# A log-sum-exp scan bound by its transfers: an opening store, a tail in rows, and no GpSimd drains

## Chip, cores, metric

One core of one Trainium2 chip. The metric is the device time of one execution in microseconds (us), lower is better.

## The reference

```python
x: (8, 4096, 2048) float32
out[:, 0, :] = x[:, 0, :]
for t in range(1, S):
    mx = np.maximum(out[:, t-1, :], x[:, t, :])
    out[:, t, :] = mx + np.log(np.exp(out[:, t-1, :] - mx) + np.exp(x[:, t, :] - mx))
```

It is a running log-sum-exp along the second axis. The kernel computes Exp, a running sum, and Ln. 268 MB are read and 268 MB written.

## The kernel before

The data go through in 64 tiles of 4 MB: 128 partitions, 4 consecutive rows of 2048 values in each (32 KB). Six buffers rotate. For every tile SyncE issues the load, ScalarE does Exp in two column halves, VectorE adds up the rows of each partition, TensorE multiplies by a triangle of ones for the sums of the partitions above and by a matrix that carries the last sum to the next tile, VectorE joins them, ScalarE does Ln and issues the store. Loads go through SyncE's DMA queue (the SP queue below), stores through ScalarE's (the ACT queue).

```python
@block.sync
def _(sp):
    def load(src, n):
        sp.dma_start(out=ti[n][:], in_=src).then_inc(loaded[n], 16)
    sp.dma_start(out=ti[0][:, 0:2, :], in_=x_v[0][:, 0:2, :]).then_inc(top, 16)
    sp.dma_start(out=ti[0][:, 2:R, :], in_=x_v[0][:, 2:R, :]).then_inc(loaded[0], 16)
    for n in range(1, NI):
        load(x_v[n], n)
    ...            # a loop: take(sp, stored[n], 16), then load the next tile into buffer n
    for n in range(NT - NI, NT):
        take(sp, stored[n % NI], 32 if n >= NT - 2 else 16)
```

`take` waits for a count on a semaphore and subtracts it. ScalarE's program, with its tail:

```python
take(act, top, 16)
act.activation(ti[0][:, 0:2, :], ti[0][:, 0:2, :], ACT.Exp)
exp(0, 0, slice(2, R))
exp(0, 1, slice(2, R))
...                # a loop of turns of six tiles: exp(n, 0), exp(n, 1), ln(n-1, 0), ln(n-1, 1), store(n-1)
for n in range(first + 1, NT):
    up, turn = n - 1, n - 1 - first
    exp(n, 0)
    if n < NT - 1:
        exp(n, 1)
    ln(up, 0, turn)
    if n == NT - 1:
        store(up, o_v[up], turn, 0)          # column half 0 of tile 62
        exp(n, 1)
    ln(up, 1, turn)
    store(up, o_v[up], turn, 1 if n == NT - 1 else None)
for h in range(2):                            # tile 63 in column halves
    ln(NT - 1, h, NT - 1 - first)
    store(NT - 1, o_v[NT - 1], NT - 1 - first, h)
settle(NT - first)
```

The softmax here doesn't subtract the row's maximum and nothing guards it: scores larger than these inputs give would overflow.

## Time and profile before

| | before |
|---|---|
| median, first three runs | 1250.71 us (1250.57 to 1251.23) |
| span of the profiled run | 1249.0 us |
| VectorE, ScalarE, TensorE busy | 82%, 73%, 52% |
| DMA | 537 MB, 430 GB/s, the DMA row 9 or more from the first slice to the 39th |

The prediction below shows the lines. The DMA share of a window can be above 1, as a packet counts with its whole duration where it starts. A DMA's semaphore goes up by 16, one step for each engine; the trace has the times of these steps, which I call landings, and they show how far the sixteen engines are apart. Neither they nor the packet records carry an engine's number: that it is one and the same engine that lands last from tile to tile (I call it the late engine), and that it is never idle, is read from how the times follow each other. And the chain of waits that the page gives ends at the last Ln, since a transfer is not an instruction: for a kernel bound by transfers it says little.

### The profile page before, as it was taken

To read this page: it belongs to the slowest core of one execution; us is meant where nothing else is said; L and a number is where in the kernel's file an instruction comes from. 1 tells how busy PE (TensorE), PEld (TensorE's weight loads), DVE (VectorE), ACT (ScalarE), POOL (GpSimd) and SP (SyncE) were. 2 spreads that over 40 slices of the span, in tenths; PEclk is the share of its full clock that TensorE was granted. 3 is DMA by queue.
4 is the path that set the end of the run, shared out by engine and by line. 5 is a ranking of instruction groups with operands and counts; after the bars stand their busy time and mean duration, and the time that the engine had idled before them with its cause. 6 is when DMAs were issued, how large, how long until landed. Compare 5 with 4: busy or idle time off the path is not lost. (4 is left out here: it accounts for less than half of the span.)

```text
span 1249.0 us, 3456 instructions
## 1 busy us (share of the span) xinstructions
PE 650.8 (52%) x960; PEld 215.3 (17%) x960; DVE 1023.0 (82%) x512; ACT 907.2 (73%) x258; POOL 1.1 (0%) x8
## 2 busy tenths in 40 slices
PE   3556455554566545655455544565545564465541
PEld 1112111111112111211111111121111121111110
DVE  4999978778787787887878878778787787877873
ACT  5897866867768677686776866867768677686774
POOL 0000000000000000000000000000000000000000
PEclk9897778786887868778778786777878878678785
DMA  9999999999999999999999999999999999999998
GB/s 403 420 436 430 433 430 437 433 431 434 430 436 434 431 433 430 437 434 430 434 430 436 436 430 434 430 436 437 428 434 431 436 436 429 434 430 436 436 430 354
DMA packets 20409, 537.01 MB, mean 430 GB/s; under 512 B 2096, under 2 KB 2096, under 8 KB 4144
## 3 DMA queue, kind: packets, MB, share of 16 engines
q1 hardware_dynamic: 9360, 268.44, 49.9%
q10 hardware_dynamic: 11040, 268.44, 49.9%
q8 instruction: 7, 0.11, 0.0%
q14 instruction: 2, 0.02, 0.0%
HBM read 268.44 MB, written 268.44 MB: 430 GB/s over the span
## 5 line engine op out<-in xcount | busy, mean ns | idle before, releaser
L136 ACT ACTIVATE ti<-ti 128x4096 f32<-128x4096 f32 (+1 forms) x128 | 452.6, 3582 | 310.2 <-ACTq L59 304.2
L232 DVE TENSOR_TENSOR ti<-ti 128x1024 f32<-128x1024 f32 x384 | 464.7, 1224 | 200.0 <-ACT ti L136 191.3
L241 DVE TENSOR_TENSOR ti<-ti,ps 128x4096 f32<-128x4096 f32 x128 | 560.0, 4416 | 9.4 <-PE ps L208 9.0
L208 PE MATMUL ps<-ti,before 128*128 128x512 f32 x512 | 380.4, 895 | 342.6 <-DVE ti L232 342.1
L142 ACT ACTIVATE ti<-ti 128x4096 f32<-128x4096 f32 x128 | 455.4, 3602 | 11.5 <-PE ps L197 6.0
L197 PE MATMUL ps<-ti,last 128*128 128x512 f32 x448 | 270.6, 735 | 234.2 <-DVE ti L241 234.2
L208 PEld LDWEIGHTS ps<-ti,before 128*128 128x128 f32 x512 | 128.7, 279 | 609.0 <-DVE ti L232 500.9
L197 PEld LDWEIGHTS ps<-ti,last 128*128 128x128 f32 x448 | 86.6, 214 | 401.8 <-DVE ti L241 334.7
L159 ACT ACTIVATE ti<-ti 128x4096 f32<-128x4096 f32 x1 | 3.6, 3616 | 6.5 <-ACTq L59 6.5
L32 ACT ACT_TABLE_LOAD x1 | 1.3, 1283 | 0.8 <-PEq L274 0.8
L103 POOL TENSOR_SCALAR_AFFINE_SELECT last<-last 128x128 f32<-128x128 f32 x1 | 0.3, 296 | 0.0
L98 POOL TENSOR_SCALAR_AFFINE_SELECT before<-before 128x128 f32<-128x128 f32 x1 | 0.3, 295 | 0.1
L95 POOL MEMSET last<- 128x128 f32 x1 | 0.2, 206 | 0.0
L94 POOL MEMSET before<- 128x128 f32 x1 | 0.2, 205 | 0.5 <-SPq L77 0.5
L274 POOL MEMSET const-bfloat16-1.0<- 128x1 bf16 x1 | 0.1, 103 | 0.0
L274 POOL MEMSET const-uint8-127<- 128x1 uint8 x1 | 0.1, 103 | 0.0
L274 POOL MEMSET const-float32-0.0<- 128x1 f32 x1 | 0.1, 99 | 0.3 <-issue 0.3
L274 POOL MEMSET const-float32-1.0<- 128x1 f32 x1 | 0.1, 99 | 0.0
## 6 DMA issues: line engine op xcount, KB each, us to landing
ti<-in_x_dram SPq DMA_DIRECT2D x63, 4096.0 KB, 38.4
out_dram<-ti ACTq DMA_DIRECT2D x62, 4096.0 KB, 44.0
out_dram<-ti ACTq DMA_DIRECT2D x4, 2048.0 KB, 12.9
ti<-in_x_dram SPq DMA_DIRECT2D x2, 2048.0 KB, 9.7
```

What stands on the lines that cost most here:

```text
L32: nc.scalar.preload_act_table_set("natural_log_exp_and_others")
L94: g.memset(before[:], 1.0).then_inc(ones, 1)
L98: g.affine_select(out=before[:], in_=before[:], compare_op=mybir.AluOpType.is_ge, fill=0.0, base=-1, pattern=[[1, P]], channel_multiplier= ...
L103: g.affine_select(out=last[:], in_=last[:], compare_op=mybir.AluOpType.is_ge, fill=0.0, base=-(P - 1), pattern=[[0, P]], channel_multiplier=1,
L136: act.activation(t[:, rows, half(h)], t[:, rows, half(h)], ACT.Exp).then_inc(exps[h], 1)
L142: act.activation(t[:, :, half(h)], t[:, :, half(h)], ACT.Ln)._wait_ge(carried[h], turn + 1).then_inc(logs, 1)
L159: act.activation(ti[0][:, 0:2, :], ti[0][:, 0:2, :], ACT.Exp)
L197: m = pe.matmul(ps[(n + 1) % 2][:, sl], last[:], ti[n % NI][:, R - 1, sl], start=True, stop=False, skip_group_check=True,)
L208: m = pe.matmul(ps[n % 2][:, sl], before[:], ti[n % NI][:, R - 1, sl], start=n % NBLK == 0, stop=True, skip_group_check=True,)
L232: a = dve.tensor_add(t[:, r, half(h)], t[:, r - 1, half(h)], t[:, r, half(h)])
L241: dve.tensor_add(t[:, :, half(h)], t[:, :, half(h)], ps[n % 2][:, half(h)].unsqueeze(1).to_broadcast([P, R, HALF]),)._wait_ge(ahead[h], n ...
L274: nc = _bacc.Bacc("TRN2", target_bir_lowering=False, num_devices=1)
```

## The change

The intent: let the ACT queue's first use happen at the head with sixteen elements, so that the first tile's store doesn't pay for it; give the last two tiles larger packets and earlier issues; drop the drains of GpSimd.

```diff
+    LAST = [slice(0, 1), slice(1, 2), slice(2, R)]
-    with tc.tile_critical():
+    with tc.tile_critical(no_gpsimd_drain=True):
-        with nc.Block() as block:
+        with nc.Block(no_gpsimd_drain=True) as block:
 ...
-                    take(sp, stored[n % NI], 32 if n >= NT - 2 else 16)
+                    take(sp, stored[n % NI], 16 * (len(LAST) if n == NT - 1 else 1))
 ...
             def _(act):
+                with nc.allow_non_contiguous_dma(reason="one element per DMA engine"):
+                    act.dma_start(
+                        out=o_v[0][0:16, 0, 0:1], in_=nc.const_aps.tensor(0.0, [16, 1], f32)
+                    ).then_inc(warm, 16)
 ...
                 take(act, top, 16)
+                take(act, warm, 16)
 ...
                 for n in range(first + 1, NT):
-                    ...                       # the tail shown above
+                    for h in range(2):
+                        exp(n, h)
+                    for h in range(2):
+                        ln(n - 1, h, n - 1 - first)
+                    store(n - 1, o_v[n - 1], 2 * (n - first))
+
+                turn = NT - 1 - first
+                ln(NT - 1, 0, turn)
+                done = 2 * turn + 1
+                for rows in LAST:
+                    ln(NT - 1, 1, turn, rows)
+                    done += 1
+                    store(NT - 1, o_v[NT - 1], done, rows)
+                settle(NT - first, done)
```

`store` takes rows instead of a column half. TensorE's program is not touched.

More of the change, by code (lines that the diff above doesn't have):

```diff
@@ L75, in take @@
         event(engine, [(s, n)], [(s, "sem-sub-imm", n)])
-    with tc.tile_critical():
+    with tc.tile_critical(no_gpsimd_drain=True):
         def sems(name, n):
             return [nc.alloc_semaphore(f"{name}{i}") for i in range(n)]
-        ones, shaped, logs, top = (
-            sems(s, 1)[0] for s in ("ones", "shaped", "logs", "top")
+        ones, shaped, logs, top, warm = (
+            sems(s, 1)[0] for s in ("ones", "shaped", "logs", "top", "warm")
         )
@@ L138, in exp, with ln, store, settle @@
                     ).then_inc(exps[h], 1)
-                def ln(n, h, turn):
+                def ln(n, h, turn, rows=slice(0, R)):
                     t = ti[n % NI]
                     act.activation(
-                        t[:, :, half(h)], t[:, :, half(h)], ACT.Ln
+                        t[:, rows, half(h)], t[:, rows, half(h)], ACT.Ln
                     )._wait_ge(carried[h], turn + 1).then_inc(logs, 1)
-                def store(n, dst, turn, h=None):
-                    cols = slice(0, D) if h is None else half(h)
-                    act.wait_ge(logs, 2 * turn + (2 if h is None else h + 1))
+                def store(n, dst, done, rows=slice(0, R)):
+                    act.wait_ge(logs, done)
                     act.dma_start(
-                        out=dst[:, :, cols], in_=ti[n % NI][:, :, cols]
+                        out=dst[:, rows, :], in_=ti[n % NI][:, rows, :]
                     ).then_inc(stored[n % NI], 16)
-                def settle(turns):
+                def settle(turns, done):
                     take(act, carried[0], turns)
                     take(act, carried[1], turns)
-                    take(act, logs, 2 * turns)
+                    take(act, logs, done)
                 take(act, top, 16)
+                take(act, warm, 16)
                 act.activation(ti[0][:, 0:2, :], ti[0][:, 0:2, :], ACT.Exp)
@@ L168, in _ @@
                         ln(n - 1, 1, n - 1)
-                        store(n - 1, o_v[bass.ds(j * NI + (n - 1), 1)][0], n - 1)
-                    settle(NI)
+                        store(n - 1, o_v[bass.ds(j * NI + (n - 1), 1)][0], 2 * n)
+                    settle(NI, 2 * NI)
                 first = turns * NI
                 for n in range(first + 1, NT):
-                    up, turn = n - 1, n - 1 - first
-                    exp(n, 0)
-                    if n < NT - 1:
-                        exp(n, 1)
-                    ln(up, 0, turn)
-                    if n == NT - 1:
-                        store(up, o_v[up], turn, 0)
-                        exp(n, 1)
-                    ln(up, 1, turn)
-                    store(up, o_v[up], turn, 1 if n == NT - 1 else None)
-                for h in range(2):
-                    ln(NT - 1, h, NT - 1 - first)
-                    store(NT - 1, o_v[NT - 1], NT - 1 - first, h)
-                settle(NT - first)
+                    for h in range(2):
[11 more added lines that the diff above has]
+                settle(NT - first, done)
             @block.tensor
```

## The prediction

> **What bounds the kernel now.** I read the page's strip of slices first, then the engines' busy shares, the DMA windows at head and tail, ScalarE's timeline at the tail and the issue list.
>
> ```profile
> PE 650.8 (52%) x960; PEld 215.3 (17%) x960; DVE 1023.0 (82%) x512; ACT 907.2 (73%) x258; POOL 1.1 (0%) x8
> ...
> DMA  9999999999999999999999999999999999999998
> GB/s 403 420 436 430 433 430 437 433 431 434 430 436 434 431 433 430 437 434 430 434 430 436 436 430 434 430 436 437 428 434 431 436 436 429 434 430 436 436 430 354
> DMA packets 20409, 537.01 MB, mean 430 GB/s; under 512 B 2096, under 2 KB 2096, under 8 KB 4144
> ```
>
> No compute engine is full, while the DMA row is 9 everywhere and the rate stands at 430 to 437 GB/s from the third slice to the 39th. 537 MB must pass and the change keeps every byte of it, so only the places where the rate falls short can give anything: the first two slices (403, 420) and the last (354). The row "under 8 KB" counts the pieces that matter at the tail: 4144 less 2096 is 2048 packets of 4 KB.
>
> The windows around the first store of a tile (ScalarE issues it at 38.46 us); the last two columns are DMA share and GB/s:
>
> ```profile
> 39.00:40.00 1.00, 0.82 (x2) 0.49 (x3) 1.00 (x2) 1.00 (x1) 0.00 (x0) 1.00 1.21 524
> 40.00:41.00 1.00, 1.00 (x3) 0.19 (x1) 1.00 (x1) 1.00 (x1) 0.00 (x0) 1.00 1.31 524
> 41.00:42.00 1.00, 0.16 (x1) 0.00 (x0) 1.00 (x1) 1.00 (x1) 0.00 (x0) 1.00 1.51 426
> 42.00:43.00 1.00, 0.00 (x0) 0.00 (x0) 1.00 (x1) 1.00 (x2) 0.00 (x0) 1.00 0.31 98
> ```
>
> A packet is counted in the window where it starts, so a window jumps between about 200 and 524; the ratio of the columns is what to read. A share of 1.21 normally buys 524 GB/s. The next three windows spend 3.13 where (524 + 426 + 98) / 524 x 1.21 = 2.42 would do: 0.71 us of all sixteen engines is lost. In the trace's packet records the loads of 32 KB in flight there take 1.3 to 2.0 us instead of 1.21, before the first store packet of the ACT queue starts; summed over 16 engines the excess is 0.70 us. No later store shows this. The only other such place is the very start of the SP queue at 2.0 to 3.5 us: first packets of 16 KB take 1.1 to 1.3 us instead of 0.61, 0.66 us per engine. So each queue's first use costs about 0.7 us of DMA time.
>
> The end of the run:
>
> ```profile
> 1230.00:1243.00 13.00, 0.00 (x0) 0.00 (x0) 2.41 (x1) 5.44 (x2) 0.00 (x0) 0.50 1.02 421
> 1243.00:1244.00 1.00, 0.00 (x0) 0.00 (x0) 0.00 (x0) 0.00 (x0) 0.00 (x0) 0.50 0.83 340
> 1244.00:1245.00 1.00, 0.00 (x0) 0.00 (x0) 0.00 (x0) 0.00 (x0) 0.00 (x0) 0.50 0.43 176
> 1245.00:1246.00 1.00, 0.00 (x0) 0.00 (x0) 0.00 (x0) 0.00 (x0) 0.00 (x0) 0.50 0.06 25
> 1246.00:1247.00 1.00, 0.00 (x0) 0.00 (x0) 0.00 (x0) 0.00 (x0) 0.00 (x0) 0.50 0.06 25
> 1247.00:1248.00 1.00, 0.00 (x0) 0.00 (x0) 0.00 (x0) 0.00 (x0) 0.00 (x0) 0.50 0.02 8
> ```
>
> A share of 0.06 is one engine in sixteen: from 1245.2 to 1247.3 a single DMA engine still writes. The sixteen increments of the last store's semaphore, in the trace, arrive at 1243.71 to 1245.47 for fifteen engines and at 1247.66 for one, and that one was 0.4 us behind the median at 8 us, 1.0 at 180, 2.1 at 760 and 3.0 at 1218. It is never idle between its first packet and 1247.33, so it is the critical path: its bytes, its stalls, and 1.7 us of semaphore and closing barriers up to the span of 1249.0.
>
> Is the last Ln on that path? ScalarE at the tail, and the issues:
>
> ```profile
> 1216.36 3.62 ACT L136 ACTIVATE ti<-ti 128x4096 f32<-128x4096 f32 x1 [0.71 <-ACT ti L142]
> 1219.88 3.60 ACT L142 ACTIVATE ti<-ti 128x4096 f32<-128x4096 f32 x1
> 1223.51 0.54 ACTq L149 DMA_DIRECT2D out_dram<-ti  x1
> 1228.21 3.62 ACT L142 ACTIVATE ti<-ti 128x4096 f32<-128x4096 f32 x1 [4.73 <-PEq L59]
> 1231.86 0.54 ACTq L149 DMA_DIRECT2D out_dram<-ti  x1
> 1232.54 3.62 ACT L142 ACTIVATE ti<-ti 128x4096 f32<-128x4096 f32 x1 [0.71 <-PEq L59]
> 1236.18 0.54 ACTq L149 DMA_DIRECT2D out_dram<-ti  x1
> ...
> out_dram<-ti ACTq DMA_DIRECT2D x4, 2048.0 KB, 12.9
> ```
>
> The last store leaves at 1236.18 and lands 11.5 us later, though 2.1 MB at 421 GB/s are 5.0 us. It stood some 6 us in line, behind bytes already queued. So the last Ln has slack.
>
> **What the Trainium skill says.** "Perfetto Trace Analysis", section "What 'DMA-bound' means", lists specific DMA engines as a first kind of bound; the windows at 25 GB/s show just that. "DMA: Bandwidth & Descriptors", section "Why a DMA increments its semaphore by 16 and not by 1", says that the engines of a transfer finish independently and only the full count means landed; the spread 1243.71 to 1247.66 agrees. Its section "Why small descriptors are slow (HBM only)" gives a fixed cost per packet; in the trace 4 KB packets follow each other every 155.3 ns, those of 16 KB every 608 and of 32 KB every 1210, that is 155.3, 152.1 and 151.3 ns for each 4 KB, which agrees: some 4 ns a packet. I found nothing in it on the first use of a queue.
>
> **The change part by part.**
>
> 1. *Tail in whole rows.* Before, tiles 62 and 63 leave as four column halves, runs of 4 KB. On each engine (8 partitions) that is 8 x 4 x 2 x 2 = 128 packets x 155.3 = 19.88 us. After, tile 62 is 8 packets of 32 KB, 8 x 1.210 = 9.68 us; tile 63 is 8 of 8 KB twice (estimate from the spacing above, 306 ns: 2 x 2.45) and 8 of 16 KB (8 x 0.608 = 4.86), 9.76 us. Sum 19.44; it saves 0.44 us on the last engine. The views agree: 421 GB/s in the tail against some 433 in the middle is 8.39 MB x (1/421 - 1/433), 0.55 us.
>
> 2. *Does the line stay full?* Tile 63's load sets Exp at 1208.53. Before, ScalarE does Exp, Ln, store, Exp, Ln; after, two Exp (to 1215.8), two Ln (to 1222.9), then the whole store of tile 62. That lifts its first half back by 7.2 us, from 1215.68 to 1222.9. Tile 61's store ends at about 1223.3 on the earliest engine and 1227.5 on the last (its increments: 1223.69 to 1227.90, less 0.35). With 1.0 us from issue to first packet, as at the head (1.03 to 2.04), early engines idle up to 0.7 us; the late one has 3.5 us of work left and doesn't notice. VectorE gets the second Exp 4 us sooner: local sums to 1219.5, joins (4.4 us each) to 1224.0 and 1228.4. Ln of half 0 is 1224.2 to 1227.8; Ln of half 1 starts near 1228.6 in pieces of 0.98, 0.98 and 1.86 us (from 3.61 for 4096 elements and 1.855 for 2048: 0.10 fixed and 0.857 per 1024). Stores go at about 1229.6, 1230.6 and 1232.4. Tile 62's bytes last until 1233 on the earliest engine and 1237 on the last, so nothing starves. The last issue comes nearly 4 us sooner and gains none of it.
>
> 3. *Opening store.* 16 elements, one packet on each engine, issued by ScalarE near 0.9 us, while the SP queue suffers its own first use. ScalarE's wait for it ends long before the load it waits for anyway (8.5 us): nothing. What it is for is the 0.71 us at 40 to 43: paid early. If its stall overlays the SP queue's, up to 0.7 is gained; if it only comes on top of the first loads, none, as the DMA engines have no slack there. I count 0.4.
>
> 4. *No GpSimd drain.* The drain of 634 ns at 1.4 us stands beside loads; that of 41 ns at 1248.0 is in the closing barrier, with one more step of SyncE (1248.17 to 1248.24): 0.05 us.
>
> TensorE is straight-line already, and its instructions are not touched. Sum: 0.44 + 0.4 + 0.05 = 0.9 us. 1250.7 - 0.9 = 1249.8.
>
> **The rivals.**
>
> - *The last issue sets the end.* The chain of waits ends in the last Ln, and moving it 3.8 us sooner would give 1247. Against it: the 6 us in line, and one engine writing alone after the others.
> - *The stall only moves to the head*, or belongs to the first large write and stays: 1250.2. The head has no idle DMA time, which speaks for it; the two first uses might run at once, which speaks against.
> - *The stall overlaps wholly*: 1249.5.
> - *Tile 62's later store starves the line.* If descriptor work takes longer than 1 us, or ScalarE runs late, the last engine could lose what the larger packets give, and more: 1251. The margin of 3.5 us speaks against.
>
> **Range and chances.** The bottom is everything working with a little extra, 1249.0; the top is no gain at the head and half of the tail's, 1250.6. Three runs of the kernel before lie within 0.7 us. 2% is 25 us, twenty times anything in sight, and bytes over rate forbid it: 537 MB at 437 GB/s are 1229 us alone.
>
> **What would show it.** 4 KB packets gone (under 8 KB some 2,100, as the semaphore writes and the sixteen elements are all that is left); tail windows back near 430 GB/s; last store issued near 1232 yet landing 13 to 15 us later; again one engine alone at the end, for about 2 us. Windows 41 to 43 at the normal ratio would show the stall gone, and the head's tells whether it moved: a first load landing later than 8.5 us means that it did. Wrong it would be if the last engine has a gap near 1224, or if another engine ends last, or if the end comes 3 us sooner.

## The result

| | before | after |
|---|---|---|
| median of six runs each, first chip | 1250.79 us (1250.57 to 1251.23) | 1250.94 us (1250.42 to 1251.32) |
| span of the profiled run | 1249.0 us | 1249.6 us |

The ratio is 1.000, with a 95% interval of 0.9987 to 1.0013: the same. Ratios here are the mean time of one kernel's fast runs over that of the other's in the same rounds, so not quite the ratio of the medians. The profiled run of after, 1251.32, happens to be the slowest of its six.

The rate and the packets on the page of after:

```profile
GB/s 403 415 435 430 433 430 436 434 433 431 431 434 436 433 431 432 432 435 434 431 433 431 435 434 433 433 431 432 436 433 432 432 431 436 434 432 431 433 432 352
DMA packets 18905, 537.01 MB, mean 430 GB/s; under 512 B 2128, under 2 KB 2128, under 8 KB 2128
```

The packets of 4 KB are gone (2128 are the semaphore writes and the sixteen elements). But the first two slices read 403 and 415 where they read 403 and 420, and the last reads 352 for 354.

The windows of after around its first tile's store, which ScalarE issues at 38.11 us (the last two columns are DMA share and GB/s):

```profile
39.00:40.00 1.00, 1.00 (x3) 0.50 (x4) 1.00 (x1) 1.00 (x1) 0.00 (x0) 0.90 1.33 524
40.00:41.00 1.00, 0.92 (x3) 0.10 (x1) 1.00 (x1) 1.00 (x1) 0.00 (x0) 1.00 2.06 524
41.00:42.00 1.00, 0.00 (x0) 0.00 (x0) 1.00 (x1) 1.00 (x1) 0.00 (x0) 1.00 0.00 0
```

Share 3.39 for 1048 GB/s, where 2.42 would do (1048 / 524 x 1.21): 0.97 us per engine is lost. In the window from 41 to 42 no packet starts on any engine. So the stall is still there. It is longer than before's 0.71, but by no more than it varies by itself (before_again, below). At the head nothing got worse: the first load lands at 8.34 us instead of 8.51.

The tail of after:

```profile
1230.00:1243.00 13.00, 0.00 (x0) 0.00 (x0) 0.46 (x1) 4.02 (x3) 0.00 (x0) 0.50 1.00 423
1243.00:1244.00 1.00, 0.00 (x0) 0.00 (x0) 0.00 (x0) 0.00 (x0) 0.00 (x0) 0.50 1.00 426
1244.00:1245.00 1.00, 0.00 (x0) 0.00 (x0) 0.00 (x0) 0.00 (x0) 0.00 (x0) 0.50 0.84 360
1245.00:1246.00 1.00, 0.00 (x0) 0.00 (x0) 0.00 (x0) 0.00 (x0) 0.00 (x0) 0.50 0.08 33
1246.00:1247.00 1.00, 0.00 (x0) 0.00 (x0) 0.00 (x0) 0.00 (x0) 0.00 (x0) 0.50 0.04 16
1247.00:1248.00 1.00, 0.00 (x0) 0.00 (x0) 0.00 (x0) 0.00 (x0) 0.00 (x0) 0.50 0.04 16
```

423 GB/s with large packets, 421 before: less is gained than forecast. One engine is again alone at the end, with packets of 16 KB that start one or two to a window. And ScalarE's timeline of after there:

```profile
1210.44 7.12 ACT L142 ACTIVATE ti<-ti 128x4096 f32<-128x4096 f32 x2 [5.30 <-ACTq L60]
1217.47 7.11 ACT L148 ACTIVATE ti<-ti 128x4096 f32<-128x4096 f32 x2
1224.61 0.34 ACTq L154 DMA_DIRECT2D out_dram<-ti  x1
1226.25 3.62 ACT L148 ACTIVATE ti<-ti 128x4096 f32<-128x4096 f32 x1 [1.67 <-PEq L60]
1230.59 1.06 ACT L148 ACTIVATE ti<-ti 128x1024 f32<-128x1024 f32 x1 [0.72 <-PEq L60]
...
1235.47 0.34 ACTq L154 DMA_DIRECT2D out_dram<-ti  x1
```

The two Exp start at 1210.44, as the last load came 1.9 us later in this run, and the last store leaves at 1235.47, only 0.7 us sooner than before. It still lands 12.7 us later, at the end of a line.

### The profile page after: what moved, and what is told of

Read it like the earlier page. It is cut to its first block, busy times and chain, and to the rows that moved or that the text cites. A ratio compares the mean times of both kernels' runs of the same rounds, so it can differ in the third digit from the quotient of the medians.

```text
span 1249.6 us, 3463 instructions
## 1 busy us (share of the span) xinstructions
PE 643.6 (52%) x960; PEld 213.2 (17%) x960; DVE 1022.8 (82%) x512; ACT 907.5 (73%) x260; POOL 1.1 (0%) x8
## 2 busy tenths in 40 slices
DMA packets 18905, 537.01 MB, mean 430 GB/s; under 512 B 2128, under 2 KB 2128, under 8 KB 2128
## 5 line engine op out<-in xcount | busy, mean ns | idle before, releaser
L142 ACT ACTIVATE ti<-ti 128x4096 f32<-128x4096 f32 (+1 forms) x128 | 452.5, 3582 | 311.9 <-ACTq L60 311.9
L214 PE MATMUL ps<-ti,before 128*128 128x512 f32 x512 | 372.9, 879 | 347.7 <-DVE ti L238 347.3
L148 ACT ACTIVATE ti<-ti 128x4096 f32<-128x4096 f32 (+1 forms) x130 | 455.8, 3549 | 8.8 <-PE ps L203 5.6
L165 ACT ACTIVATE ti<-ti 128x4096 f32<-128x4096 f32 x1 | 3.6, 3616 | 6.4 <-ACTq L60 6.4
## 6 DMA issues: line engine op xcount, KB each, us to landing
out_dram<-ti ACTq DMA_DIRECT2D x1, 2048.0 KB, 12.7
```

The source lines that it names most:

```text
L142: act.activation(t[:, rows, half(h)], t[:, rows, half(h)], ACT.Exp).then_inc(exps[h], 1)
L148: act.activation(t[:, rows, half(h)], t[:, rows, half(h)], ACT.Ln)._wait_ge(carried[h], turn + 1).then_inc(logs, 1)
L214: m = pe.matmul(ps[n % 2][:, sl], before[:], ti[n % NI][:, R - 1, sl], start=n % NBLK == 0, stop=True, skip_group_check=True,)
```

## The experiments

Theory of the prediction (P): 0.4 us from the opening store, 0.44 from the tail, 0.05 from the drains, on the path of one late engine. Theory after reading the two traces (T): the stall belongs to the first tile's store, not to the queue's first use, so the opening store gives nothing; the tail gives 0.26; the closing barrier costs 0.07. Eighteen kernels ran, on four chips, each with its own runs of before.

### The parts alone

**Only the opening store.** Edit: the kernel before with the opening store and `take(act, warm, 16)` of the diff above.

> The kernel before with the opening store and ScalarE's wait for it, nothing else. Prediction's theory (the stall at 40 to 43 us belongs to the first use of the ACT queue, and is paid early): 0.4 to 0.7 us faster, windows 40 to 43 at the normal ratio. Theory from the trace of after (the stall belongs to the first real store, whatever went before): within 0.2 us of before, with 0.7 to 1.0 us per engine still lost between 39 and 43 us. Rival: the opening store makes that stall longer, 0.2 to 0.4 us slower.

Measured: 1250.89 us (1250.58 to 1250.97), before 1251.03. Its windows:

```profile
40.00:41.00 1.00, 1.00 (x3) 0.19 (x1) 1.00 (x1) 1.00 (x1) 0.00 (x0) 1.00 1.39 524
41.00:42.00 1.00, 0.04 (x1) 0.00 (x0) 1.00 (x1) 1.00 (x1) 0.00 (x0) 1.00 1.53 459
42.00:43.00 1.00, 0.00 (x0) 0.00 (x0) 1.00 (x1) 1.00 (x1) 0.00 (x0) 1.00 0.21 66
```

3.13 of share for 1049 GB/s, so 0.71 us lost: the stall of before's first profile. The opening store neither removes nor lengthens it.

**Only the tail.** Edit: the change without `warm` and without the drain flags.

> The kernel before with the new tail alone (tile 62 whole, tile 63 in rows 1, 1, 2). Prediction: 0.44 us faster, from packets. Theory from the two traces: from the last landing of tile 61 to the last landing of all it takes 19.50 us instead of 19.76, so 0.26 faster. Rival: the early engines' pause near 1224 costs, and nothing is gained.

Measured: 1250.51 us, and its six runs lie between 1250.47 and 1250.57, below every run of before in that call (lowest 1250.62). The ratio, 0.9989 with an interval of 0.9975 to 1.0003, is still called the same, as four of before's eleven runs took 1252 to 1256. From tile 61's last landing to the last of all: 1227.84 to 1247.35, 19.51 us.

**Only the drains.** Edit:

```diff
-    with tc.tile_critical():
+    with tc.tile_critical(no_gpsimd_drain=True):
-        with nc.Block() as block:
+        with nc.Block(no_gpsimd_drain=True) as block:
```

> The kernel before without the two GpSimd drains. Prediction: 0.05 us faster. Theory from the two traces: SyncE's drain and its count become two instructions, so from the last landing to the end it takes 1.44 us instead of 1.37, 0.07 us slower; neither is to be seen in the medians, so the profile's stretch decides.

Measured: 1251.09 us (1250.7 to 1251.23). The line of the block in the kernel before, for SyncE (count, then duration in ns, first and last start in us):

```profile
L90 SPq DRAIN  x1: 7/7/7, 1247.7 to 1247.7; - x1
L90 SPq EVENT_SEMAPHORE  x1: 17/17/17, 1247.9 to 1247.9; - x1
```

and in this kernel:

```profile
L90 SPq EVENT_SEMAPHORE  x2: 17/17/17, 1247.9 to 1248.1; - x2
L90 SPq DRAIN  x1: 7/7/7, 1247.9 to 1247.9; - x1
```

In before the drain itself raises the barrier's count; without the GpSimd drain a second instruction does. From the last landing to the span's end it takes 1.44 us instead of 1.37. GpSimd's own drain of 634 ns is gone, but it stood at 1.4 us beside loads.

**The whole change again.** No edit.

> The changed kernel unaltered, on the same chip as its parts. If the parts add up, its distance from before is the sum of the three. Theory from the traces: between 0.4 us faster and 0.2 slower, with the same stall at 39 to 43 us. If the profiled run of after was merely one of the slow ones of a spread of 0.9 us, this profile ends nearer 1249.0.

Measured: 1250.65 us (1250.45 to 1250.92), ratio 0.999 (0.9975 to 1.0004), stall 0.97 us, 19.51 us for the tail, 1.44 us for the close, span 1249.2. The first profile of after was indeed of the longest of its six runs.

**Before against itself**. No edit.

> The kernel before against itself: the noise. Ratio 1.000 with an interval like the others'; the stall at the first store may be 0.7 or 0.97 us per engine, as both values came up in kernels that share this part.

Measured: 1250.95 us in both, ratio 0.9999 (0.9986 to 1.0012). But its stall is 0.94 us, where the first profile of the very same kernel had 0.70. The table puts the profiles side by side; the stall is the excess of packet durations between 35 and 48 us over 16 engines, "tile 61" the last and the median landing of its store, "tail" from that last landing to the last of all, "close" from there to the span's end.

| kernel | stall | tile 61, last | tile 61, median | tail | close |
|---|---|---|---|---|---|
| before | 0.70 | 1227.90 | 1224.86 | 19.76 | 1.37 |
| before_again | 0.94 | 1228.13 | 1225.18 | 19.77 | 1.37 |
| open_only | 0.69 | 1227.72 | 1224.88 | 19.75 | 1.37 |
| drain_only | 0.98 | 1228.04 | 1225.08 | 19.76 | 1.44 |
| tail_only | 0.96 | 1227.84 | 1225.08 | 19.51 | 1.37 |
| after | 1.00 | 1228.64 | 1225.25 | 19.50 | 1.44 |
| after_again | 0.97 | 1228.24 | 1225.11 | 19.51 | 1.44 |

The last two columns repeat to 0.02 us and follow the code. The first three don't. In these seven profiles the stall is 0.7 or some 0.97, and the median landing of tile 61 follows it (1224.87 against 1225.08 to 1225.25). But the kernels below that share this part fill the gap and go beyond it: 0.51 (extra16), 0.74, 0.77, 0.91; and cols63, with 0.74, has its median at 1225.20. So it is a spread, not two sizes. The late engine adds 2.8 to 3.4 us of its own. Before and before_again, one program, are 0.23 us apart by then, after and after_again 0.40.

### What the stall belongs to

Before's single trace could not tell three things apart, as they happen at one moment: the ACT queue's first bulk use, the first bulk write to HBM, and the first store with an address computed in a loop. The next four kernels ran once each, so their state is unknown and their times say little; the stall is read inside each trace.

**Fixed addresses.** Edit: the first turn of ScalarE's loop written out, `o_v[n - 1]` instead of `o_v[bass.ds(...)]`.

> The kernel before with the first turn of ScalarE's loop written out, so that the first six stores have fixed addresses and not ones computed in the loop. If the stall comes from the computed address: none near 40 us. Else 0.7 to 1.0 as before.

Measured: one run of 1250.63 us; 0.77 us lost near 40 us. Not the address.

**A load on the ACT queue.** Edit:

```diff
-                sp.dma_start(out=ti[0][:, 2:R, :], in_=x_v[0][:, 2:R, :]).then_inc(loaded[0], 16)
 ...                                        # in ScalarE's program, first:
+                act.dma_start(out=ti[0][:, 2:R, :], in_=x_v[0][:, 2:R, :]).then_inc(loaded[0], 16)
```

> The kernel before with the second half of tile 0 loaded by ScalarE's queue instead of SyncE's, so that the ACT queue carries 2 MB in bulk at the head. If the stall belongs to the first bulk use of that queue, there is none near 40 us. If it belongs to the first writes of bulk to HBM: 0.7 to 1.0 us per engine near 40 as before.

Measured: one run of 1251.17 us. The first tile's store is issued at 42.97, and the windows after it:

```profile
44.00:45.00 1.00, 0.78 (x2) 0.00 (x0) 1.00 (x1) 1.00 (x1) 0.00 (x0) 1.00 1.05 426
45.00:46.00 1.00, 0.00 (x0) 0.00 (x0) 1.00 (x1) 1.00 (x1) 0.00 (x0) 1.00 1.87 524
46.00:47.00 1.00, 0.00 (x0) 0.00 (x0) 1.00 (x2) 1.00 (x2) 0.00 (x0) 1.00 0.11 33
```

3.03 of share for 983 GB/s, which need 2.27: 0.76 us lost, though the queue had carried 2 MB in bulk since 1 us. This is the run that refutes P's reading: it is not the queue's first use, small (open_only) or in bulk.

**The first store on SyncE's queue.** Edit: as peel, but tile 0's store is issued by SyncE, behind its loads, when ScalarE has raised a semaphore.

> As peel, but tile 0's store is issued on SyncE's queue, behind its loads, so that the ACT queue starts with tile 1's near 55 us. If the stall belongs to the ACT queue's start: none until 55, then 0.7 to 1.0 us per engine. If it belongs to the start of bulk writing whatever the queue: at the SP queue's store near 58 us or at the ACT queue's near 55, whichever is first, and not at the other.

Measured: one run of 1254.83 us (the loads that follow wait for that store). ScalarE's first store, tile 1's, leaves at 54.39, and is the first bulk write, as SyncE's waits in line:

```profile
56.00:57.00 1.00, 1.00 (x3) 0.19 (x1) 1.00 (x1) 1.00 (x1) 0.00 (x0) 1.00 1.30 524
57.00:58.00 1.00, 0.22 (x1) 0.00 (x0) 1.00 (x1) 1.00 (x1) 0.00 (x0) 1.00 1.83 524
58.00:59.00 1.00, 0.00 (x0) 0.00 (x0) 1.00 (x1) 1.00 (x2) 0.00 (x0) 1.00 0.00 0
```

0.71 us lost (3.13 less 2.42), and nothing near 40. SyncE's store, some microseconds later, shows no stall of its own. Here the ACT queue's start and the first bulk write coincide again; with act_load together, the start of bulk writing is what is left. One rival stays open: every stall seen comes at a write of the ACT queue, and in no run does SyncE's queue write first, so it could belong to that queue's first write alone.

**Two probes ahead.** Edit: the sixteen elements issued at 8.5 us, after the first load; then 1 MB of zeros from a spare tile to `o_v[0][:, 0, :]` at 13.84 us; both waited for.

> The kernel before with two more stores by ScalarE ahead of the first real one, both overwritten later: 16 elements at 8.5 us, 1 MB of rows of 8 KB at some 13.4 us, each waited for, so that the ACT queue is empty again before the first tile's store at 38 us. If the stall belongs to the first bulk write of the ACT queue, 0.7 to 1.0 us per engine is lost near 15 us and nothing near 40. If it comes at every start of store traffic beside loads: it is lost both times. If it belongs to the first whole tile: only near 40. The 16 elements: no loss under any.

Measured: one run of 1253.09 us. The sixteen elements show no loss. The megabyte: 0.31 us per engine lost between 15 and 23 us, and 0.38 at the first tile's store, near 46. Neither theory had this: part is paid early, and the sum, 0.69, is what the others lose at once. The probe is 2.2 us slower, about what a megabyte takes at 430 GB/s (2.4). So the loss can be moved, but the two sums suggest that it isn't saved by it. It also means that the very first bulk write doesn't pay for all. What both places share is that the store queue was empty before: the megabyte had landed when the first tile's store was issued. In the traces of before and of open_64k_late every later store is issued before the one ahead of it has landed on any engine, and there the loads of no later store lose more than 0.03 us. A start of stores from an empty queue, beside loads, fits all these traces; no run was made to test it.

**A larger opening store.** Edit: instead of the sixteen elements, 64 KB (512 B in each of 128 partitions) once GpSimd has written the source, near 2.0 us, waited for before the first Exp.

> The kernel before with an opening store of 64 KB over all 128 partitions near 2 us instead of 16 elements. If the stall at 40 us is the price of the first write of any size by each port or partition, it is gone: up to 0.6 us faster. If it is paid by bulk, as in probe: less than 0.1 us of it is gone and 0.15 us is added; the same within noise.

Measured: 1286.52 us (1282.39 to 1287.79), ratio 1.028 (1.0264 to 1.0297). Its rate:

```profile
GB/s 394 432 425 422 430 424 422 425 427 424 419 425 426 421 425 424 421 422 425 421 424 417 423 423 423 425 422 425 417 426 420 424 431 423 424 422 429 427 343 285
```

The line is lower from the third slice on, 417 to 431 up to the 38th where before has 428 to 437. In the packet records of most tiles' periods loads of 32 KB are held up, by 0.1 to 0.6 us per engine each time (22 us in sum, so not all of the 36), and some engines more than others: on tile 60's store the first engine lands 24 us ahead of the last, on tile 61's the median engine 14.8 us. ScalarE waits for all sixteen landings of a load, so all go slower. Most of these stores were issued while the one ahead was still under way on every engine, so an empty store queue isn't the whole story of such losses.

**The same DMA, waited for later.** Edit: the same, with `take(act, warm, 16)` after the three first Exp.

> open_64k with the same DMA, but ScalarE waits for it only after its first three Exp, so the first tile's compute is no longer 3.4 us late. If the 36 us came from that delay (the phase of stores against loads): within 0.5 us of before. If they come from the DMA itself (128 more descriptors on the queue, or bytes written early): some 36 us slower again.

Measured: 1251.86 us (1251.71 to 1252.2) against 1250.99, and 0.83 us of stall near 40. The 36 us are gone, so the DMA itself doesn't make them. But 0.87 us remain, more than the 0.5 expected, and not all of it is accounted for. The first Exp waits until 12.1 us in open_64k and starts near 8.6 here; but in act_load and probe it waits until 13.6, and their stores start later still (at 43 and 45 us; 40.3 in open_64k), without that loss. What exactly the delay must meet is open. And no larger opening store pays.

### What sets the end

These kernels ran in other calls than tail_only, most on other chips. tail_only was 0.52 us below the before, 1251.03; the before of relief, tail_whole and cols63 was 1250.95, that of extra16 and extra15 1250.74, and that of extra8 and extra7 1250.99.

**Tile 63 in one store.** Edit: `LAST = [slice(0, R)]`.

> As tail_only, but tile 63 leaves in one store after both Ln, near 1236. The early engines run out of bytes near 1234 and idle 2 us or more; the late engine has bytes until 1237.5. If the late engine alone sets the end: within 0.15 us of tail_only. If the last issue or all engines together set it: 1 to 2 us slower.

Measured: 1250.46 us (1250.37 to 1252.55), as tail_only's 1250.51, though ScalarE issues the store only after both Ln. It left at 1233.59, sooner than I had estimated, as ScalarE no longer stops between pieces. The pieces of the change buy nothing: the bytes were in line already. In this trace two engines end late together, at 1247.46 and 1247.66, the next at 1245.09; so it is not always one.

**Tile 63 in column halves.** Edit: tail_only with tile 63 as in the kernel before.

> As tail_only, but tile 63 leaves in column halves, packets of 4 KB, as in the kernel before. If the 0.3 us of tail_only comes from the packets of tile 62 and 63 alike: about 0.15 us slower than tail_only. If the pieces and their order matter and not the packets: no difference, or the whole 0.3.

Measured: 1250.83 us (1250.66 to 1251.57), from 1228.17 to 1247.72 19.55 us, between tail_only's 19.51 and before's 19.76. The larger part of the 0.25 us came with tile 62. This is one profile, and the difference of 0.04 is at the limit of what they repeat to.

**Sparing the last engine.** Edit, on tail_only: rows 0, 1 and 2 as whole rows, and row 3 as two stores:

```diff
+                for parts in (slice(0, 120), slice(120, P)):
+                    act.dma_start(
+                        out=o_v[NT - 1][parts, 3:R, :], in_=ti[(NT - 1) % NI][parts, 3:R, :]
+                    ).then_inc(stored[(NT - 1) % NI], 16)
```

> As tail_only, but the last row of tile 63 leaves as 120 partitions (a count that spreads over fifteen engines[...]) and 8 partitions (over eight). If one late engine sets the end and it is the sixteenth, it is spared eight packets of 8 KB, 2.45 us: the end is then set by the fifteen others, which finished 2.3 us earlier, with 0.3 us more to write; 1.8 to 2.1 us faster than tail_only, all landings within 0.7 us. If the late engine is one of the first eight: 0.3 us slower. If it is another: the same. If the end is set by the rate of all engines together: the same.

Measured: 1251.44 us, 0.9 slower than tail_only. It doesn't answer the question. The packets of 8 KB between 1242 and 1245 us took 413 to 541 ns on average instead of some 310. A possible cause is that 120 partitions, if they go eight to an engine in a row, make engines share ports of the on-chip memory: the Trainium skill, "SBUF — State Buffer", section "Door 1: The DMA port swizzle", gives each port two groups of four partitions, 32 apart. No run here tests that cause.

**An extra load on some of the engines.** The landings show that it goes to k engines, one packet of 24 KB each. That these are always the lowest-numbered, so that each set lies within the next, is an assumption that no trace here can check. Edit, on tail_only, in SyncE's last loop, with k = 16, 15, 8 or 7:

```diff
+                    if n == NT - 4:
+                        sp.dma_start(
+                            out=ti[0][0:4*k:4, 0:3, :], in_=x_v[0][0:4*k:4, 0:3, :]
+                        ).then_inc(loaded[0], 16)
+                take(sp, loaded[0], 16)
```

> As tail_only, with one more load near 1218 us that nothing uses: 24 KB in each of 16 partitions, which spreads over all sixteen engines, one packet of some 0.9 us each. The late engine has no slack, so the end comes later by the packet: 0.9 us, up to 1.8 if engines share a port. Rival (the tail is bound by the last issue): no change.

Measured: 1252.28 us (1251.89 to 1254.02).

> As extra16 with 15 partitions instead of 16, which spreads over the fifteen [...]engines; the sixteenth gets nothing. If the sixteenth is the late engine and alone sets the end: within 0.15 us of tail_only, though fifteen engines do the same extra work. If the late engine is another, or all engines together set the end: later by as much as extra16.

Measured: 1251.97 us (1251.96 to 1252.07). The late engine needs 11.2 us from tile 60's landing to tile 61's instead of tail_only's 9.76, so it has the extra packet too. The engine without it is the one that lands first (1224.34, the next 1225.43), and not the late one. Its number is not in the trace.

> As extra7 with 8 partitions, so the eighth engine is added. If the late engine is the eighth: extra7 leaves the time alone and extra8 costs 0.9 to 1.5 us. If it is the ninth to fifteenth: both leave it. If it is one of the first seven or all engines count: both cost.

Measured: 1251.62 us (1251.57 to 1251.88), 1.1 more than tail_only. The late engine needs 10.67 us, one packet of 0.91 more; the close is 1.45, one more wait. Together 0.99.

> As tail_only, with one more load of 24 KB in each of 7 partitions near 1218 us, which spreads over the seven [...]engines. If one late engine alone sets the end and is not one of these seven: within 0.15 us of tail_only, though seven engines do 0.9 us more. If it is one of them, or all engines together set the end: 0.9 to 1.5 us later, as extra15.

Measured: 1251.82 us (1251.61 to 1256.63), as extra8. But the profile fell on the run of 1256.63, in which four engines were late already at tile 60, three by 5 to 6 us and one by 9; that one needs 9.68 us, no extra packet, and the three others 10.6 to 10.9. Times and trace point to different engines; which one is late is not settled, nor whether it is always the same. The landings show that one engine ends 2.2 to 3.1 us after all others in extra16, extra15 and extra8 (extra8: 1248.70, the next 1245.59), and 1.9 to 2.5 us after them in the seven profiles of the table; these four runs agree that it sets the end but do not exclude the rival, that all engines together do.

## Why the prediction was wrong

It said 1249.8 (1249.0 to 1250.6); 1250.94 was measured, and 1250.65 on the second chip.

1. **The step that failed is part 3, the opening store**, and under it the sentence "So each queue's first use costs about 0.7 us of DMA time". I had two stalls and two first uses, and took the coincidence for the cause. The 0.4 us that I counted is 0: the stall is 0.71 us in open_only, and comes where bulk writing starts, with 2 MB on the queue beforehand (act_load: 0.76) as without. The rival that I named in half a sentence, that it "belongs to the first large write and stays", held for this change. Why there is a stall at all stays open, and probe shows that a later start of stores can pay part of it.

2. **Part 4 had the wrong sign**: not 0.05 us faster but 0.07 slower, the same in drain_only, after and after_again. I looked for the instruction that goes and not for what must take over the count that another one raised.

3. **Part 1 was right in kind and mis-sized**: 0.25 us for 0.44. Before's tail took 19.76 where 128 packets of 155.3 ns make 19.88. Tile 62 whole took 9.75 (after: 1228.64 to 1238.39) where I had 9.68: I used 1210 ns from the middle, where loads and stores alternate, for a stretch that only stores (median duration of a 32 KB packet there 1220 ns in after, 1213 in the middle). The rows took 9.75 where I had 9.76.

4. **Part 2, the slack**, was right where it mattered. The last issue was 3 us later than forecast, as the last load was 1.9 us later, pieces of Ln took 1.06 us for 0.98, and there are 0.4 us between them; none of it reached the end. More idle time than the 0.7 us that I allowed fell on the early engines: the fifteen landings of tile 62, which spread over 1.9 us in before, came within 0.4 us in after, since they had all waited for the store of 1224.61 and started together. The late engine had work throughout.

5. **What remains is the noise**, which I had under-rated. The measured terms make 0.25 - 0.07 = 0.18 us where I had 0.89: 0.40 of the difference is the opening store, 0.19 the tail, 0.12 the drains. 1250.8 less 0.18 is 1250.6, the very edge of my range. One program varies by 0.2 to 0.4 us before its tail even starts, by the size of the stall and the late engine's drift. That is as much as the whole gain.

A small misreading besides: the rate from the third slice to the 39th is 428 to 437 GB/s, not 430 to 437; nothing rests on it.

The version that the runs favour is tail_only: the tail's 0.25 us without the close's 0.07. By the traces it is the best of the three, by times the same as both.

## What to carry to other kernels

When every byte is in line from the first microsecond to the last, count what stands on the last DMA engine; issuing the last store in pieces, the first of them sooner, changed nothing here (1250.46 in one store, 1250.51 in three). One stall that coincides with a first use isn't yet the cost of that use: move the use without the stall's other companions (here: a load on that queue) before building on it. Take a packet's time from a stretch with the same mix of loads and stores as the one that is to change, and compare two profiles of one program before believing tenths.

## What the Trainium skill lacked or had wrong

- "DMA: Bandwidth & Descriptors" has nothing on the stall where bulk writes start beside bulk reads: 0.51 to 1.00 us on every engine in the profiles with one such start, whether the queue had been used before or not, and 0.31 and 0.38 in the one with two. Whether it needs the ACT queue is not known from these runs.
- The same page, section "Latency and other measured facts", calls engines 7 and 15 usually slower and, as its best guess, ties it to descriptors made by GpSimd's software. Here all data move through the queues of SyncE and ScalarE, and still one engine is 3.0 us behind the median at 1218 us, and the next ones aren't; in the one profiled run of 1256.63 us it was 9 us. The traces have no engine numbers, so whether it is 7 or 15 is not shown.
- The same page, section "Why small descriptors are slow (HBM only)", has the right direction for 4 KB against 8 to 32 KB, but its worked example is for 256 B; the size in a stretch of stores alone is 19.51 against 19.76 us for 8.39 MB.
- No page has it that leaving out the GpSimd drain makes the closing barrier longer: 1.44 us instead of 1.37.
- No page warns that waiting for one early store of 64 KB before the first tile's compute, 3.5 us later then, can cost 36 us (1286.52 with the wait there, 1251.86 with it later), in good part by loads that are held up in most periods; the condition for it is not known from these runs.
